# Moving the scaling and transposes of state-space tiles between hops, and dropping one tile of the convolution column, in a hybrid decoder layer

## The chip, the cores and the metric

The kernel runs on one core of one Trainium2 chip. The core has TensorE (PE in the profile, with its weight loads as PEld), VectorE (DVE), ScalarE (ACT), GpSimd (POOL) and SyncE (SP), which issues nearly all transfers. The metric is the device time in microseconds of one execution. A profiled execution is a separate one and has a time of its own.

## The reference

One layer with `S = 2048` tokens and a model width of 1024, in float32. The input is normalized and modulated, projected in one matrix, and split into two groups of heads: attention in a sliding window, and a Mamba-2 state-space group (SSD). The outputs of both are concatenated and projected back; then follows a SwiGLU network. The part that the change touches is the second group:

```python
xbc = silu(causal_depthwise_conv(xbc, conv_w, conv_b))      # four taps along the tokens
xs, Bm, Cm = split(xbc, ...)
...                                                          # chunks of 128 tokens
cb = einsum('bclgn,bcsgn->bclsg', Cc, Bc)
y_diag = einsum('bclsg,bclsgj,bcsgjp->bclgjp', cb, decay, xdt)
states = einsum('bclgn,bclgj,bclgjp->bcgjpn', Bc, decay_to_end, xdt)
...                                                          # prev: the state carried from chunk to chunk
y_off = einsum('bclgn,bcgjpn,bclgj->bclgjp', Cc, prev, exp(a_cs))
y = (y_diag + y_off).reshape(b, s, SSM_HEADS, SSM_HEAD_DIM)
y = y + xf * d_skip[:, None]
y = y * silu(z)
yg = y.reshape(b, s, SSM_GROUPS, 256)
y = yg * rsqrt(mean(yg * yg, axis=-1) + EPS) * ssm_norm_w
out = concatenate([attn, y]) @ w_out
```

## The kernel before, in words

The tokens are worked in four blocks of 512, each of four tiles of 128. A block goes through the projections for query, key, value, convolution (`convolved`) and gate (`gated`), then through attention and the state space, then through the output projection (`out_proj`). The SwiGLU part fills the rest of the span, from about 700 us on, and the mixing of the last two blocks runs beside its beginning.

**Dense work and sides.** The projections are the dense work. A product in float32 is made of three matmuls of split operands (L286 to L288); a column of the convolution takes 24 matmuls, in two pieces of 12 with a `yield` behind each. They write into four PSUM banks named `d`. Attention (`attentions`) and the state space (`ssds`) are sides: Python generators whose `yield`s cut them into hops. After each piece of dense work `tick(ratio)` adds a ratio to a counter, `due`, and issues one hop for each whole unit in it. The ratios are MIX, MIX2 and MIX1. `both` alternates the hops of attention and of the state space. So the program's text, by the order of pieces and hops, sets the order of the instructions of PE, which is kept as written. On the other engines a scheduler orders the instructions with list priorities; hops are issued at high priority (`urgent`), and `behind(engine)` puts an instruction after the last one of an engine issued so far. In the trace an engine's instructions run in that order, so one that waits holds up those behind it.

**The banks of the sides.** The sides have one PSUM bank each for the names `am`, `at`, `sm` and `st`. A state-space tile of 128 tokens uses `st` for its input transposes (L764), for the transposes of B (L778), for the product with the carried state, `yo` (L797), for the new state (L806), and for the transposes of the finished tile (L751 in `turned`). It uses `sm` for the C times B products (L771), for the decays (L735 and L736, with the exponent L738 on ACT and the product L740 on DVE), and for the diagonal part, `yd` (L818). So a matmul into `st` waits until the last reader of the bank before it is done: for L751 this reader is ACT's L754.

**A tile's end.** After L818 DVE adds and gates (L820, L821), ACT squares (L825), and a reciprocal root is found in steps, on POOL for three tiles of a block and on DVE for the last (L249 to L266). Its result scales the tile (`normed`, L746 on ACT), PE transposes the scaled tile (`turned`, L751), ACT evicts it (L754), and SP stores it to `mix`. The finished tile of one step is scaled and turned during the hops of the next step; the last of a block at the block's end.

**The convolution column.** `convolved` computes 8 columns of 128 channels. For each, ACT copies the bank (L507), ACT makes the first tap (L510), DVE adds the fourth from the bank and so frees it (L511), ACT and DVE make the two other taps (L512, L513), POOL adds both (L514). Half a column later `end` takes the tanh on ACT (L499), combines it on DVE (L501) and stores the column (L502 on SP). The tiles come from rings, whose oldest tile is reused when its last reader is done: `s` of three tiles (two per column before), shared with `gated`, and `sx` of two. At L278 ACT rounds weights, at L368 it squares the input of a later block's norm.

**The end of block 1.** The mixing of block 1 (`mix1`) runs beside dense work of blocks 2 and 3 with ratio MIX1. `finish(mix1)` issues all hops that are left, one behind the other, without dense work between. `mixed` loads the mixed tiles back for the output projection and splits them (L848 on ACT, L849 on DVE).

Of the kernel before, what the change touches and what calls it, by code (L numbers as in the profile page):

```python
# [22 lines left out]
T = 512  # L23
# [7 lines left out]
NEG = -1e30  # L31
RAW, SPLIT = 5, 6
TMP, M1, M2, M4 = 8, 3, 8, 4
MIX, MIX2, MIX1, RATIO_UP = 0.78, 1.1, 1.25, 0.75
URGENT = 1000
HALF = 32
ROPE_THETA = 10000.0
# [8 lines left out]
def hymba_layer(ctx, tc, xT, xtok, pos, wada, wadk, vecs, rows, wq, wkv, wz, wx, wo, wgu, wd, outT):  # L46
# [11 lines left out]
    def big(tag, bufs, dt=F32, pool=sb):  # L58
        return pool.tile([P, T], dt, name=tag, tag=tag, bufs=bufs)
# [434 lines left out]
    def convolved(b, h):  # L494
        ending = []

        def end(c, cv, th, o):
            with behind(mybir.EngineType.Activation):
                nc.scalar.activation(th, cv, AF.Tanh)  # L499
            with behind(mybir.EngineType.DVE):  # L500
                nc.vector.scalar_tensor_tensor(o, th, 1.0, cv, ALU.add, ALU.mult)  # L501
            nc.sync.dma_start(xs_d[b][c], o)  # L502

        def evicted(c, ps):
            cin = small([P, T + 3], "cin", 2, pool=ip)
            nc.gpsimd.tensor_copy(cin[:, 0:3], halo[:, c, :])
            nc.scalar.copy(cin[:, 3:T + 3], ps)  # L507
            nc.gpsimd.tensor_copy(halo[:, c, :], cin[:, T:T + 3])
            cv, th, o = big("s", 3, pool=fw), big("s", 3, pool=fw), big("sx", 2, pool=ip)
            nc.scalar.activation(cv, cin[:, 0:T], AF.Identity, scale=conv_w[:, c, 0:1], bias=conv_b[:, c:c + 1])  # L510
            nc.vector.scalar_tensor_tensor(cv, ps, conv_w[:, c, 3:4], cv, ALU.mult, ALU.add)  # L511
            nc.scalar.activation(th, cin[:, 1:1 + T], AF.Copy, scale=conv_w[:, c, 1:2])  # L512
            nc.vector.scalar_tensor_tensor(th, cin[:, 2:2 + T], conv_w[:, c, 2:3], th, ALU.mult, ALU.add)  # L513
            nc.gpsimd.tensor_tensor(cv, cv, th, ALU.add)  # L514
            return c, cv, th, o

        for c in range(8):
            ps = dense()
            for half in range(2):
                if half:  # L520
                    if ending:
                        end(*ending.pop())
                    yield
                whi, wlo = weight(wx[c, half], T, ("x", c, half), b == 1)
                for i in range(4):
                    k = 4 * half + i
                    ws = slice(i * P, (i + 1) * P)
                    mm3(ps, whi[:, ws], wlo[:, ws], h[k][0], h[k][1], k == 0, k == KT - 1)
            with urgent():
                ending.append(evicted(c, ps))  # L530
            if c == 7:
                end(*ending.pop())
            yield
# [176 lines left out]
    def ssds(b, stepping, m):  # L710
        def load(t):
            xl = m.m4().bitcast(F32).rearrange("p h t -> p (h t)").rearrange("p (c t) -> p c t", c=8)
            z, ts = m.m2(), slice(t * P, (t + 1) * P)
            nc.sync.dma_start(xl, xs_d[b][:, :, ts].rearrange("c p t -> p c t"))
            nc.sync.dma_start(z, z_d[b * NT + t])
            return [xl[:, c, :] for c in range(8)], z
# [7 lines left out]
        def factors(t, g):  # L724
            hs, u = slice(4 * g, 4 * g + 4), m.m4()
            uhi, ulo = u[:, 0, :], u[:, 1, :]
            nc.vector.tensor_tensor(uhi.rearrange("p (h l) -> p h l", h=4), ub,
                                    ahi[:, t, hs].bitcast(F32).unsqueeze(2).broadcast_to([P, 4, P]), ALU.mult)
            nc.gpsimd.tensor_tensor(ulo.rearrange("p (h l) -> p h l", h=4), ub,
                                    alo[:, t, hs].unsqueeze(2).broadcast_to([P, 4, P]), ALU.mult)  # L730
            return uhi, ulo

        def decays(u, cbt):
            sg = bank("sm", 1)
            nc.tensor.matmul(sg, later_r, u[0], start=True, stop=False)  # L735
            nc.tensor.matmul(sg, later_r, u[1], start=False, stop=True)  # L736
            dm = m.m2()
            nc.scalar.activation(dm, sg, AF.Exp)  # L738
            d3 = dm.rearrange("p (h l) -> p h l", h=4)
            nc.vector.tensor_tensor(d3, d3, cbt.unsqueeze(1).broadcast_to([P, 4, P]), ALU.mult)  # L740
            return dm
# [6 lines left out]
        def turned(y, o, ts):  # L748
            ps = bank("st", 1)
            for c in range(4):  # L750
                nc.tensor.transpose(ps[:, c * P:(c + 1) * P], y[:, c * P:(c + 1) * P], ident)  # L751
            o3 = o.rearrange("p (c t) -> p c t", c=4)
            for c in range(4):
                nc.scalar.activation(o3[:, c, :], ps[:, c * P:(c + 1) * P], AF.Copy, scale=snw[:, c:c + 1])  # L754
            nc.sync.dma_start(dst[4:8, :, ts].rearrange("c p t -> p c t"), o3)

        for t in range(NT):
# [22 lines left out]
            nc.scalar.copy(btok, ps[:, 0:2 * P])  # L780
            ms = [decays(u, cbt[:, 0, :])]
            u = factors(t, 1)
            if out:
                normed(out[0], out[3])
            yield
            if out:
                turned(*out[:3])
                yield
            ms.append(decays(u, cbt[:, 1, :]))
            if t + 1 < NT:  # L790
                nxt = load(t + 1)
            old = carry["state"]
            if old is not None:
                y = m.m2()
                yo = bank("st", 1)
                for g in range(2):
                    nc.tensor.matmul(yo[:, g * 256:(g + 1) * 256], x[6 + g], old[:, g * 256:(g + 1) * 256],  # L797
                                     start=True, stop=True)
                nc.vector.tensor_tensor(by_head(y), by_head(yo), bc64(ecs), ALU.mult)
                nc.gpsimd.tensor_tensor(y, y, xsd, ALU.add)  # L800
            else:
                y = xsd
            yield
            st = bank("st", 1)
            for g in range(2):
# [23 lines left out]
            rsqrt(rs, ss, 2, nc.vector if t == NT - 1 else nc.gpsimd, "rss", sb)  # L829
            out = (y, o, ts, rs)  # L830
            yield
        yield
        normed(out[0], out[3])
        yield
        turned(*out[:3])
        yield

# [671 lines left out]
    def finish(last):  # L1509
        while last in sides:  # L1510
            if next(sides[0], sides) is sides:
                sides.pop(0)
# [25 lines left out]
    def take(g, n):  # L1538
        for _ in range(n):
            next(g)  # L1540

    with tc.manual_schedule(engines={mybir.EngineType.PE}):
# [42 lines left out]
        h = nxt  # L1585
        run(queries(3, h), MIX1)
        run(keys_values(3, h), MIX1)
        mix = []
        finish(mix1)
        sides.append(attentions(2, common))  # L1590
        conv = convolved(3, h)
        widening.close()
        early = ctx.enter_context(ExitStack())
        bp = early.enter_context(tc.tile_pool(name="b0", bufs=1, reuse_waits="tile"))
# [1 line left out]
        ops = {}  # L1596
        operand_tiles(ops, bp, ("b11",), 12)
        for i in range(6):
            take(conv, 1)
            tick(0.5)  # L1600
            if i > 1:
                next(split, None)
            if i == 1:
                dg = diagonal(y_of[0])
            if i == 3:
                bcs = [spread(y_of[0], bc=side_bank(2), dg=dg)]
# [205 lines left out]
```

## Time and profile before

| what | value |
|---|---|
| time, median of 3 runs | 2202.72 us (2201.24 to 2203.47) |
| profiled execution, its own time | 2204.92 us |
| its span, first to last instruction | 2203.2 us |
| mean granted clock of TensorE | 0.987 |
| ACT busy | 1014.0 us (46%) |
| POOL busy | 550.6 us (25%) |
| share of PE in the chain that ended last | 84% |

The profile gives the busy time of each engine, a line of slices of the span, the chain of work that ended last, and groups of instructions with what ended the idle time before them. A row of the timeline gives the start, the duration, the engine, the line of the kernel and the tiles written and read; in brackets stand the idle time of the engine ahead of it and the instruction that released it. "PE d L286 <- DVE s L511" reads: PE's matmul of line 286, into a bank of `d`, waited for DVE's instruction of line 511, which writes a tile of the ring `s`. The granted clock is the share of TensorE's full speed that it was allowed.

### The profile page before, as it was taken

Reading aid. Unit: us, or ns where it says so; the run is one execution under the profiler, and the core shown is the slowest. Engines: PE = TensorE matmul, PEld = TensorE weight load, DVE = VectorE, ACT = ScalarE, POOL = GpSimd, SP = SyncE. Lnnn points to the kernel's source line nnn. Section 1 sums busy time; section 2 is a strip of 40 time slices with the busy share of each in tenths; the row PEclk is TensorE's granted clock in tenths of the full one; section 3 lists DMA queues with packets and bytes.
Section 4 is the critical chain, followed back from the end, with each engine's and each line's share of the span. In section 5 each row is a group of like instructions: output and inputs, shape, how many; then the busy total and the mean of one; then the engine's idle time right before and its main releaser. Section 6 shows DMA issues by size and latency. Waiting matters only on the chain.

```text
span 2203.2 us, 33249 instructions
## 1 busy us (share of the span) xinstructions
PE 2149.3 (98%) x10984; PEld 1771.8 (80%) x10984; DVE 1661.3 (75%) x3195; ACT 1014.0 (46%) x2135; POOL 550.6 (25%) x658
## 2 busy tenths in 40 slices
PE   8989998999999999999999999999999999999998
PEld 6878896878778677788888788788888888788887
DVE  7978856786668877688888668878888775786575
ACT  3675734653545654443334445533333334554441
POOL 0214432322102211153341221323332321210011
PEclk8999999999999999999999999999999999999999
DMA  7788987796998522333334577735555436678553
GB/s 284 245 298 308 360 260 260 248 360 205 344 345 297 167 90 87 125 106 117 117 116 164 196 264 268 271 127 189 173 165 191 158 120 224 233 264 278 182 163 103
DMA packets 287708, 466.76 MB, mean 212 GB/s; under 512 B 27440, under 2 KB 97072, under 8 KB 287536
## 3 DMA queue, kind: packets, MB, share of 16 engines
q1 hardware_dynamic: 286960, 464.13, 62.7%
q8 instruction: 86, 1.41, 0.3%
q14 instruction: 86, 0.70, 0.1%
q10 hardware_dynamic: 576, 0.52, 0.1%
HBM read 329.73 MB, written 134.81 MB: 211 GB/s over the span
## 4 chain that ended last, share of the span: by engine, by line
PE 84%; DVE 7%; DMA 5%; issue 2%; ACT 2%; POOL 1%; SPq 0%; DVEq 0%; ACTq 0%; POOLq 0%
PE d L1179 18%; PE d L1049 9%; PE d L1048 9%; PE d L1047 9%; PE d L286 6%; PE d L288 6%; PE d L287 6%; PE d L1320 1%; PE am L1049 1%; PE am L1047 1%; PE am L1048 1%; PE am L706 1%; PE sm L1049 1%; PE sm L1047 1%; PE sm L1048 1%
## 5 line engine op out<-in xcount | busy, mean ns | idle before, releaser
L1179 PE MATMUL d<-a,w 128*128 128x512 f32 x1716 | 403.7, 396 | 3.0 <-DVE w L1175 2.1
L1179 PEld LDWEIGHTS d<-a,w 128*128 128x128 f32 x1716 | 321.9, 188 | 81.9 <-DVE w L1175 2.9
L1049 PE MATMUL d<-b,w 128*128 128x512 f32 x924 | 368.1, 399 | 1.4 <-DVE w L896 1.4
L1048 PE MATMUL d<-b,w 128*128 128x512 f32 x924 | 368.5, 399 | 0.2 <-DVE b L930 0.2
L1047 PE MATMUL d<-b,w 128*128 128x512 f32 x924 | 366.5, 400 | 1.7 <-ACT w L895 0.9
L1047 PEld LDWEIGHTS d<-b,w 128*128 128x128 f32 x924 | 175.1, 189 | 41.9 <-ACT b L929 1.6
L1049 PEld LDWEIGHTS d<-b,w 128*128 128x128 f32 x924 | 174.7, 189 | 42.2 <-DVE w L896 2.1
L1048 PEld LDWEIGHTS d<-b,w 128*128 128x128 f32 x924 | 175.3, 190 | 41.3 <-DVE b L930 0.9
L895 ACT ACTIVATE w<-s 128x512 fp32r<-128x512 f32 x176 | 111.0, 631 | 206.1 <-PE d L1049 152.7
L286 PE MATMUL d<-w,hl 128*128 128x256 f32 (+1 forms) x592 | 173.7, 293 | 6.9 <-DVE s L511 6.5
L287 PE MATMUL d<-w,hl 128*128 128x256 f32 (+1 forms) x592 | 168.3, 284 | 0.0
L288 PE MATMUL d<-w,hl 128*128 128x256 f32 (+1 forms) x592 | 168.2, 284 | 0.0
L896 DVE TENSOR_TENSOR w<-s,w 128x512 fp32r<-128x512 f32 x176 | 156.7, 891 | 10.1 <-ACT w L895 9.4
L895 ACT ACTIVATE w<-raw 128x512 fp32r<-128x512 f32 x132 | 83.4, 632 | 151.7 <-PE d L1049 62.1
L1161 DVE TENSOR_TENSOR a<-a 128x512 fp32r<-128x512 f32 x154 | 108.0, 714 | 51.6 <-ACT a L1160 51.2
L1175 DVE TENSOR_TENSOR w<-raw,w 128x512 fp32r<-128x512 f32 x156 | 115.4, 749 | 41.0 <-ACT w L1174 40.8
L296 POOL TENSOR_TENSOR acc<-acc,t 128x512 f32<-128x512 f32 x35 | 53.3, 1523 | 355.8 <-ACT t L295 346.0
L1160 ACT ACTIVATE a<-a 128x512 fp32r<-128x512 f32 x154 | 95.4, 628 | 86.2 <-DMA a<-act_t 48.5
L286 PE MATMUL d<-hl,w 128*128 128x512 f32 x320 | 133.2, 416 | 0.0
L288 PE MATMUL d<-hl,w 128*128 128x512 f32 x320 | 127.0, 397 | 0.3 <-DVE w L279 0.3
L287 PE MATMUL d<-hl,w 128*128 128x512 f32 x320 | 126.7, 396 | 0.0
L1174 ACT ACTIVATE w<-raw 128x512 fp32r<-128x512 f32 x156 | 90.2, 587 | 78.7 <-PE d L1179 53.0
(421 smaller groups left out, 4778.2 us busy)
## 6 DMA issues: line engine op xcount, KB each, us to landing
raw<-in_wgu_dram SPq DMA_DIRECT2D x176, 256.0 KB, 2.9
act_t<-t SPq DMA_DIRECT2D x88, 256.0 KB, 3.1
a<-act_t SPq DMA_DIRECT2D x88, 256.0 KB, 4.4
act_b<-t SPq DMA_DIRECT2D x66, 256.0 KB, 2.0
a<-act_b SPq DMA_DIRECT2D x66, 256.0 KB, 4.5
aw<-in_wada_dram SPq DMA_DIRECT2D x64, 256.0 KB, 4.9
w<-w_x SPq DMA_DIRECT2D x32, 512.0 KB, 6.0
raw<-wd_s SPq DMA_DIRECT2D x64, 256.0 KB, 3.1
```

Source lines behind the costliest of these rows:

```text
L286: nc.tensor.matmul(out, ahi, bhi, start=first, stop=False)
L287: nc.tensor.matmul(out, ahi, blo, start=False, stop=False)
L288: mm3.last = nc.tensor.matmul(out, alo, bhi, start=False, stop=last)
L895: nc.scalar.activation(hi, x, AF.Copy)
L896: eng.tensor_tensor(lo, x, hi.bitcast(F32), ALU.subtract)
L1047: nc.tensor.matmul(out, ahi, bhi, start=first and k == 0, stop=False, skip_group_check=True)
L1048: nc.tensor.matmul(out, ahi, blo, start=False, stop=False, skip_group_check=True)
L1049: mm3.last = nc.tensor.matmul(out, alo, bhi, start=False, stop=k == 3, skip_group_check=True)
L1160: nc.scalar.activation(hi, raw, AF.Copy)
L1161: nc.vector.tensor_tensor(lo, raw, hi.bitcast(F32), ALU.subtract)
L1175: nc.vector.tensor_tensor(w[1], raw, w[0].bitcast(F32), ALU.subtract)
L1179: mm3.last = nc.tensor.matmul(ps, w[x][:, ws], act[k][y], start=new and k == 0 and x + y == 0, stop=k == KP - 1 and x == 1, skip_group_che ...
```

## The change

The diff makes four edits.

1. In `ssds` the scaling of the tile before (`normed`) moves a hop later, to stand with the product with the carried state (`yo`), and `turned` a hop later again, to stand with the second decay and the load of the next tile. A tile's hops were: input; B, first decay and `normed`; `turned`; second decay, load and `yo`; new state; diagonal part. They are: input; B and first decay; `normed` and `yo`; `turned`, second decay and load; new state; diagonal part. The first tile of a block, which has no tile before it, has one hop more. At a block's end two hops pass before `normed` and two before `turned`, where one did.
2. In `convolved` the tile `th` is gone. The taps two and three and the tanh are computed in place in `o`, which comes from the ring `sx` of two. The ring `s` of three holds one tile per column in place of two.
3. MIX1 goes from 1.25 to 1.5.
4. In place of `finish(mix1)` stands a loop that takes pieces of the fourth block's convolution, with a tick after each, as long as `mix1` has hops; pieces taken there are left out of the six that follow.

```diff
-MIX, MIX2, MIX1, RATIO_UP = 0.78, 1.1, 1.25, 0.75
+MIX, MIX2, MIX1, RATIO_UP = 0.78, 1.1, 1.5, 0.75
...
-        def end(c, cv, th, o):
+        def end(c, cv, o):
             with behind(mybir.EngineType.Activation):
-                nc.scalar.activation(th, cv, AF.Tanh)
+                nc.scalar.activation(o, cv, AF.Tanh)
             with behind(mybir.EngineType.DVE):
-                nc.vector.scalar_tensor_tensor(o, th, 1.0, cv, ALU.add, ALU.mult)
+                nc.vector.scalar_tensor_tensor(o, o, 1.0, cv, ALU.add, ALU.mult)
...
-            cv, th, o = big("s", 3, pool=fw), big("s", 3, pool=fw), big("sx", 2, pool=ip)
+            cv, o = big("s", 3, pool=fw), big("sx", 2, pool=ip)
...
-            nc.scalar.activation(th, cin[:, 1:1 + T], AF.Copy, scale=conv_w[:, c, 1:2])
-            nc.vector.scalar_tensor_tensor(th, cin[:, 2:2 + T], conv_w[:, c, 2:3], th, ALU.mult, ALU.add)
-            nc.gpsimd.tensor_tensor(cv, cv, th, ALU.add)
-            return c, cv, th, o
+            nc.scalar.activation(o, cin[:, 1:1 + T], AF.Copy, scale=conv_w[:, c, 1:2])
+            nc.vector.scalar_tensor_tensor(o, cin[:, 2:2 + T], conv_w[:, c, 2:3], o, ALU.mult, ALU.add)
+            nc.gpsimd.tensor_tensor(cv, cv, o, ALU.add)
+            return c, cv, o
...
             u = factors(t, 1)
+            yield
             if out:
                 normed(out[0], out[3])
-            yield
-            if out:
-                turned(*out[:3])
-                yield
-            ms.append(decays(u, cbt[:, 1, :]))
-            if t + 1 < NT:
-                nxt = load(t + 1)
             old = carry["state"]
             if old is not None:
                 y = m.m2()
...
             else:
                 y = xsd
+            yield
+            if out:
+                turned(*out[:3])
+            ms.append(decays(u, cbt[:, 1, :]))
+            if t + 1 < NT:
+                nxt = load(t + 1)
             yield
             st = bank("st", 1)
...
-        yield
+        for _ in range(2):
+            yield
         normed(out[0], out[3])
-        yield
+        for _ in range(2):
+            yield
         turned(*out[:3])
...
-        mix = []
-        finish(mix1)
+        mix, conv, begun = [], convolved(3, h), 0
+        while mix1 in sides:
+            take(conv, 1)
+            tick(1.0)
+            begun += 1
         sides.append(attentions(2, common))
-        conv = convolved(3, h)
...
         for i in range(6):
-            take(conv, 1)
+            if i >= begun - 2:
+                take(conv, 1)
             tick(0.5)
```

Three places show how the instructions move. The numbers in the names tell tiles apart; "..." stands for dense matmuls left out, and a line of the changed kernel is about two higher than the same line before, from L845 on, or six lower for `yo` (L791 for L797).

The first is the end of the first block's convolution on ACT: the copy L507, the taps L510 and L512, with the weights' rounding L278, the norm's squares L368 and, of the attention, L624 and L631. Before:

```order
L278 ACTIVATE w<-raw 128x512
L368 ACTIVATE t,ssq<-t 128x512
L507 COPY cin<-d 128x512
L278 ACTIVATE w<-raw 128x512
L624 CAST k_ring<-am 128x128
L368 ACTIVATE t,ssq<-t 128x512
L631 ACTIVATE m_1569<-at 128x512
L368 ACTIVATE t,ssq<-t 128x512
L499 ACTIVATE s<-s 128x512
L368 ACTIVATE t,ssq<-t 128x512 x2
L512 ACTIVATE s<-cin,vec 128x512
L510 ACTIVATE s<-cin,vec 128x512
```

And with the change:

```order
L512 ACTIVATE sx<-cin,vec 128x512
L507 COPY cin<-d 128x512
L278 ACTIVATE w<-raw 128x512
L510 ACTIVATE s<-cin,vec 128x512
L278 ACTIVATE w<-raw 128x512
L512 ACTIVATE sx<-cin,vec 128x512
L368 ACTIVATE t,ssq<-t 128x512
L278 ACTIVATE w<-raw 128x512
L368 ACTIVATE t,ssq<-t 128x512
L624 CAST k_ring<-am 128x128
```

The last column's copy and taps now stand ahead of the squares and of the attention's copies, and the tap L510 ahead of L512.

The second is the last tile of block 0. On PE, before, the transposes of the tile before it (`m_3919`) and of the tile itself (`m_4545`):

```order
L751 MATMUL st<-ident,m_3919 128x128 x4
...
L735 MATMUL sm<-m_4336,later_r 128x512
L736 MATMUL sm<-m_4336,later_r 128x512
L797 MATMUL st<-state,m_3915 128x256 x2
...
L806 MATMUL st<-m_4225,m_4328 128x256 x2
...
L818 MATMUL sm<-m_4223,m_4333 128x64 x4
L818 MATMUL sm<-m_4223,m_4542 128x64 x4
...
L751 MATMUL st<-ident,m_4545 128x128 x4
```

With the change the same tiles are `m_3883` and `m_4512`:

```order
L791 MATMUL st<-state,m_4009 128x256 x2
...
L751 MATMUL st<-ident,m_3883 128x128 x4
L735 MATMUL sm<-m_4454,later_r 128x512
L736 MATMUL sm<-m_4454,later_r 128x512
...
L806 MATMUL st<-m_4300,m_4446 128x256 x2
L818 MATMUL sm<-m_4298,m_4451 128x64 x4
L818 MATMUL sm<-m_4298,m_4560 128x64 x4
...
L751 MATMUL st<-ident,m_4512 128x128 x4
```

Between the last L818 and the last L751 stood 24 dense matmuls and now stand 60. The transposes of the tile before moved the other way, to 12 dense matmuls ahead of L806, and L806 and L818 have none between them. The same place on ACT, with the change (`m_4178` is the tile that L751 of `m_3883` transposes into, `m_4560` the decay that the second L818 reads):

```order
L499 ACTIVATE sx<-s 128x512
L850 ACTIVATE hl_5240<-hl_5240 128x512
L507 COPY cin<-d 128x512
L754 ACTIVATE m_4178<-st,vec 128x128 x4
L850 ACTIVATE hl_5242<-hl_5242 128x512
L738 ACTIVATE m_4560<-sm 128x512
L510 ACTIVATE s<-cin,vec 128x512
```

Before, both L754 of that tile and the exponent L738 stood ahead of the first split (L848, now L850); now they stand behind the first and the second.

The third is a tile of block 1 that has one before it, on PE. Before, from the diagonal part of a tile to its transposes (`m_6105`), the attention's hops (L623, L628, L663, L697) left out where they only repeat:

```order
L818 MATMUL sm<-m_5890,m_6098 128x64 x4
...
L764 MATMUL st<-ident,m_6101 128x128 x4
L771 MATMUL sm<-m_6101 128x128 x2
...
L778 MATMUL st<-ident,m_6101 128x128 x2
L735 MATMUL sm<-m_6323,later_r 128x512
L736 MATMUL sm<-m_6323,later_r 128x512
...
L697 MATMUL at<-ident,m_5839 128x128 x4
L751 MATMUL st<-ident,m_6105 128x128 x4
```

With the change (`m_6061`):

```order
L818 MATMUL sm<-m_5905,m_6115 128x64 x4
...
L764 MATMUL st<-ident,m_6118 128x128 x4
L771 MATMUL sm<-m_6118 128x128 x2
...
L778 MATMUL st<-ident,m_6118 128x128 x2
...
L706 MATMUL am<-m_6379,v_ring 64x256 x4
...
L791 MATMUL st<-state,m_6118 128x256 x2
...
L751 MATMUL st<-ident,m_6061 128x128 x4
L735 MATMUL sm<-m_6403,later_r 128x512
```

The product with the carried state and the second decay changed places around L751, and 72 dense matmuls stand between L818 and L751 where 48 stood.

## The prediction

> **What bounds the kernel now.** I read the page's busy times and its clock line first, then the waits of PE, then windows, then the timeline at the longest waits.
>
> ```profile
> PE 2149.3 (98%) x10984; PEld 1771.8 (80%) x10984; DVE 1661.3 (75%) x3195; ACT 1014.0 (46%) x2135; POOL 550.6 (25%) x658
> PEclk8999999999999999999999999999999999999999
> ```
>
> TensorE is busy for 98% of the span, and the change adds and removes no matmul. So the time can only move by TensorE's waits and by what the clock does around them. Busy time includes matmuls at half clock, which is why 98% hides some of the loss. In the waits the columns are total, count and longest.
>
> ```profile
> PE st L751 <- ACT m L746: 11.8, 2, 7.5
> PE d L286 <- DVE s L511: 6.5, 1, 6.5
> ...
> PE d L287 <- DVE b L849: 1.6, 2, 1.3
> ```
>
> The two longest lines stand where the change edits: the transposes of a finished SSD tile (L751) wait for its scaling (L746), and a projection (L286) waits for a conv column's eviction (L511). The windows show the price (columns: width; PE, PEld, DVE, ACT, POOL busy; granted clock; DMA share; GB/s).
>
> ```profile
> 100.00:150.00 50.00, 42.13 (x276) 37.68 (x276) 42.06 (x106) 37.64 (x90) 11.82 (x17) 0.93 0.80 279
> 350.00:400.00 50.00, 42.48 (x203) 33.90 (x203) 35.12 (x80) 24.77 (x59) 16.05 (x20) 0.90 0.67 222
> 450.00:500.00 50.00, 50.00 (x284) 40.10 (x284) 40.10 (x90) 26.30 (x68) 11.24 (x21) 1.00 0.98 346
> 500.00:550.00 50.00, 45.49 (x356) 42.18 (x355) 28.95 (x122) 18.15 (x53) 14.39 (x34) 0.97 0.64 207
> 700.00:750.00 50.00, 45.28 (x199) 33.79 (x199) 39.13 (x74) 29.42 (x68) 12.43 (x9) 0.86 0.60 201
> ```
>
> TensorE idles 7.9, 7.5, 4.5 and 4.7 us in four of these windows, and in the same four the clock is below 1. Only the first three lie at what is edited.
>
> **Change part by part.** It moves hops; the instructions of a tile stay the same. The tanh tile of the conv is gone as a name, not as work.
>
> *(a) The last tile of block 0.* The rows are of PE, ACT and DVE.
>
> ```profile
> 348.52 1.89 PE L818 MATMUL sm<-m,m 128*128 128x64 f32 x16
> 363.52 1.11 PE L751 MATMUL st<-ident,m 128*128 128x128 f32 x4 [7.53 <-ACT m L746]
> 369.46 0.39 PE L286 MATMUL d<-hl,w 128*128 128x512 f32 x1
> 369.69 0.40 PE L287 MATMUL d<-hl,w 128*128 128x512 f32 x1
> ...
> 348.12 0.63 ACT L848 ACTIVATE hl<-hl 128x512 fp32r<-128x512 f32 x1 [5.57 <-DMA hl<-mix]
> 362.96 0.91 ACT L746 ACTIVATE m<-m,rs 128x256 f32<-128x256 f32 x2 [3.87 <-DVE rs L266]
> 364.67 1.15 ACT L754 ACTIVATE m<-st,vec 128x128 f32<-128x128 f32 x4 [0.28 <-PE st L751]
> 342.06 1.51 DVE L740 TENSOR_TENSOR m<-m,m 128x512 f32<-128x512 f32 x1
> ```
>
> L751 was due at 363.52 − 7.53 = 355.99. Behind the wait the clock is half until about 369.3 (the 0.90 of the window; from 369.46 on matmuls start 0.23 us apart again): of the 5.8 us from 363.52 to there half is lost, 2.9. Together 10.4 us. Now 60 dense matmuls stand between L818 and L751 where 24 stood: 36 × 0.23 = 8.3 us more, against 7.53 needed. This wait goes, with 0.8 us to spare.
>
> But something is late next. L751 of the tile before now stands 12 dense matmuls ahead of L806, which takes the same single bank (st) and so waits until ACT's L754 has emptied it. On ACT that L754 stands behind L850 (L848 of before), which the 348.12 row shows waiting 5.57 us for a transfer. If this lands as before: 348.12 + 0.63 (L850) + 0.57 (the conv copy) + 1.15 (L754), less overlap, gives about 350.3, while L806 is due about 1 us ahead of 348.52. That is a wait of 2.8. Then L818 needs DVE's L740, whose exponent (L738) stands on ACT behind a second L850: 350.3 + 0.6 + 0.6 + 1.5 = 353.0, while L818's second half is due near 352.3 or before: 0.7 to 2.7, taken as 1.8. New stall 4.6; at half clock behind it for 3.4 us another 1.7. Queued behind both is all of TensorE. Term (a): −7.5 − 2.9 + 4.6 + 1.7 = **−4.1** (from −10.4 if the transfer lands 5 us sooner, to 0 if it lands 4 us later).
>
> *(b) A tile of block 1.*
>
> ```profile
> 489.94 1.89 PE L818 MATMUL sm<-m,m 128*128 128x64 f32 x16
> 508.63 0.90 PE L751 MATMUL st<-ident,m 128*128 128x128 f32 x4 [4.26 <-ACT m L746]
> ...
> 508.07 0.91 ACT L746 ACTIVATE m<-m,rs 128x256 f32<-128x256 f32 x2 [0.97 <-POOL rs L261]
> ```
>
> L751 was due at 504.4. From the end of L818 (491.8) to that of L746 (509.0) the chain over POOL's root takes 17.1 us. Now 72 dense matmuls instead of 48 lie between L818 and L751, 24 × 0.23 = 5.5 us more, over 4.26: the wait goes, with the clock's part (0.03 of 50 us, 1.5, or 3.4 us at half, 1.7). I leave 0.5 for the closer rows around it. Term (b): **−5.5** (−6.0 to −4).
>
> *(c) The conv column at 122.*
>
> ```profile
> 115.75 0.28 PE L286 MATMUL d<-w,hl 128*128 128x256 f32 x1
> 129.11 0.58 PE L286 MATMUL d<-w,hl 128*128 128x256 f32 x1 [6.47 <-DVE s L511]
> ...
> 120.44 0.63 ACT L368 ACTIVATE t<-t 128x512 f32<-128x512 f32 x1 [1.31 <-DMA t<-in_xtok_dram]
> 121.55 0.63 ACT L278 ACTIVATE w<-raw 128x512 fp32r<-128x512 f32 x1
> 127.47 0.80 ACT L510 ACTIVATE s<-cin,vec 128x512 f32<-128x512 f32 x1
> 128.31 0.75 DVE L511 SCALAR_TENSOR_TENSOR s<-d,vec,s 128x512 f32<-128x512 f32 x1
> ```
>
> The column's matmuls are done near 116, yet L510 runs at 127.47: ahead of it on ACT stand L368, which waits for a transfer, and L512, which waits for a tile of the three-tile ring. L286 was due at 122.64. In the new order L507 comes ahead of L368, and between it and L510 stands one L278. At worst that runs where it does now: 121.55 + 0.63 + 0.80 + 0.75 = 123.7, a stall of 1.1; with the hand-overs 1.5, and 0.8 for a short half clock. Of 6.47 + 2.35 (4.7 us at half, from 129.1 to 133.8, in which the 0.93 of the window lies) = 8.8 remain 2.3. Term (c): **−6.5** (−8.8 to −3).
>
> *(d), (e) The last hops of block 2's projections and the denser ticks.* With MIX1 at 1.5 every second tick issues two hops beside `gated(2)`, `out_proj(0)`, `queries(3)` and `keys_values(3)`, so that block 1's mixing is used up before `finish(mix1)` stood. The loop in its place therefore runs no conv piece (`mix1` has left `sides`), and `begun` stays 0: the edit along conv pieces costs and brings nothing by itself. What `finish` packed together waited, and the loads behind it too:
>
> ```profile
> 556.61 1.08 PE L706 MATMUL am<-m,v_ring 128*64 128x256 f32 x8 [0.88 <-ACT m L699]
> ```
>
> With part of the 1.6 us of L849 above, −1.9. Against it stand two hops at one tick (L706 waiting for L699 as here: two or three times 0.9) and ACT queued behind an L512 that now waits for a store; I take **+2.0**, from 0 to +8. The region from 741 us on keeps its order nearly to the row; the idle of 700 to 750 I leave unchanged, ±4.
>
> *The ring of two.* The column's third tap and tanh now live in `o`, so L512 of a column waits until the store of the column two before has landed, instead of DVE's L511 and L501 of columns before.
>
> ```profile
> 201.82 0.59 ACT L507 COPY cin<-d 128x512 f32<-128x512 f32 x1 [4.46 <-PE d L288]
> 217.27 0.59 ACT L507 COPY cin<-d 128x512 f32<-128x512 f32 x1
> 219.21 0.71 ACT L512 ACTIVATE s<-cin,vec 128x512 f32<-128x512 f32 x1
> ...
> 231.49 1.02 SPq L502 DMA_DIRECT2D xs<-sx  x1
> ...
> DMA to landing us min/median/max: 2.0/5.2/8.3
> ```
>
> Two columns take 217.27 − 201.82 = 15.45 us; a tile of `o` would be held from 219.21 until 231.49 + 5.2 = 236.69, 17.5 us. But the half column's delay of tanh is in it, TensorE has four banks ahead, and L510 and L511, which free the bank, now need only the other ring. I cost it within (e), and its failure as a rival.
>
> Sum: −4.1 − 5.5 − 6.5 − 1.9 + 2.0 = −16.0. The profiled execution took 2204.9, the span's 2203.2 and 1.7 outside it, 2.2 above the median of the runs; so 2188.9 as a profile and **2187** as a median.
>
> On the clock a rule speaks. These rows stand ahead of half clock in the 700 window:
>
> ```profile
> 699.13 0.50 PE L1047 MATMUL d<-b,w 128*128 128x512 f32 x1 [0.92 <-ACT w L895]
> 701.33 0.79 PE L1049 MATMUL d<-b,w 128*128 128x512 f32 x1 [0.38 <-DVE w L896]
> 702.35 0.63 PE L1048 MATMUL d<-b,w 128*128 128x512 f32 x1
> 702.78 0.63 PE L1049 MATMUL d<-b,w 128*128 128x512 f32 x1
> ```
>
> Matmuls start 0.43 us apart after waits of 0.92 and 0.38, so short waits in a row of small matmuls can halve the clock too; that is why I charge 1.7 behind the split stall of (a). The Trainium skill, page "TensorE: Matmul & The Clock Gate", section "Why this matters for your kernels", warns of idle gaps over about 3 us alone. By that rule the stall of (a), split into 2.8 and 1.8, would keep the clock and the time would be 2185; the row disagrees with the rule here.
>
> **The rivals.** *No new waits:* if the transfer ahead of L850 lands sooner and the ticks of two hops find their operands, everything named goes: −10.4 − 6.0 − 8.8 − 2.5 = −27.7, 2175. For it: those transfers are issued by the same hops and the DMA share is 0.67 there. Against: two hops now share a tick at the place of (a).
>
> *Given back to the transfers:* the stages before 650 us move 200 to 350 GB/s, with a DMA share of 0.98 in 450 to 500. Where TensorE gains, weights may come no sooner, and a wait for raw weights takes each gain's place: 2199 to 2203. Against: in that very window TensorE is busy for all 50.00 us.
>
> *The ring of two sets the pace (slower):* 17.5 − 15.45 = 2.0 us per pair of columns, three pairs a block, four blocks: +24; with the −16 and the cover of four banks lost, up to 2211. It decides from the point where a store lands later than 3.2 us after its issue in a column that has no slack; the median is 5.2. It would show as L286 <- L511 in every block. Against: 4.46 us of ACT's idle ahead of L507 in the row above, which is slack the ring may use.
>
> **How the numbers follow.** The likeliest case, with 2181 to 2195 from the bounds of (a), (c) and (e), has 0.62; no new waits 0.14; given back 0.13; the ring 0.11. A measurement of this kernel can tell about 0.2%, 4.4 us, from no change. Faster than that: 0.62 + 0.14 and a little of the third, 0.79; the same 0.12; slower 0.09, since the ring's loss may stay below the gain. The range for eight in ten reaches from the second case to the third: 2175 to 2200.
>
> **What would show it.** Right: no L751 <- L746 over 1 us among the waits of PE, a clock of 0.97 or more in 350 to 400 and 500 to 550, L286 <- L511 at 122 below 2 us, and L806 or L818 with a wait of 2 to 5 us near 347. Wrong: L512 waiting for `sx` over 2 us in most columns with L511 among PE's releasers; a new line of PE for `raw` or `w`; or the last TURN at later than its 60 rows.

## The result

| | before | changed |
|---|---|---|
| median of 6 runs | 2202.51 us (2201.24 to 2203.9) | 2190.07 us (2188.52 to 2192.3) |
| profiled execution, its own time | 2204.92 us | 2188.96 us |
| its span | 2203.2 us | 2186.9 us |

The ratio is 0.9942, with a 95% interval of 0.9932 to 0.9952. The forecast was 2187 us. The medians differ by 12.4 us and the two profiled executions by 16.0, because the profile before was 2.4 us above its median and the one after 1.1 below. The terms of the prediction were worked out from profiles, so they are held against the profiles below; by the medians, some 3.5 us of what those show belong to these two executions and not to the change.

The page after, its busy times and clock:

```profile
PE 2140.5 (98%) x10984; PEld 1763.5 (81%) x10984; DVE 1669.6 (76%) x3195; ACT 1017.8 (47%) x2137; POOL 547.5 (25%) x658
PEclk8999999999999999999999999999999999999999
```

As many matmuls, 8.8 us less of busy time: they ran less at half clock. The waits of PE after (total, count, longest):

```profile
PE am L663 <- DVE k_ring L625: 4.8, 2, 4.7
...
PE d L1049 <- ACT t L1081: 3.0, 1, 3.0
PE d L286 <- DVE s L511: 2.7, 1, 2.7
PE at L628 <- DMA m<-q: 2.4, 2, 2.1
...
PE st L806 <- ACT m L754: 0.4, 1, 0.4
```

L751 for L746, the longest wait of before (11.8 us), is not among them. L511's has fallen from 6.5 to 2.7. New are the scores (L663) waiting for the split of the keys (L625) and, at 711 us, L1049; the wait for a load of queries (L628) has grown from 0.9 to 2.1. The windows after:

```profile
100.00:150.00 50.00, 43.42 (x299) 38.58 (x298) 47.20 (x126) 39.41 (x94) 13.16 (x15) 1.00 0.95 328
350.00:400.00 50.00, 48.22 (x284) 40.70 (x282) 37.85 (x90) 31.71 (x74) 16.93 (x24) 1.00 0.81 272
400.00:450.00 50.00, 45.83 (x295) 38.94 (x295) 40.02 (x99) 29.48 (x78) 12.69 (x21) 0.97 0.80 266
500.00:550.00 50.00, 50.00 (x392) 46.27 (x390) 28.92 (x125) 16.40 (x48) 11.61 (x28) 1.00 0.79 264
700.00:750.00 50.00, 46.82 (x229) 35.52 (x230) 44.70 (x81) 32.05 (x73) 14.74 (x11) 0.97 0.52 169
```

The clock, 0.93, 0.90, 0.97 and 0.86 in four of these windows before, is 1.00 in three and 0.97 in that from 700. What is gained from 350 to 400 and from 500 to 550 is partly lost again in the window from 400 to 450, whose TensorE was busy for 48.2 us at full clock before.

Where the 16.3 us of the span went is seen from the same instruction in both traces (starts in us):

| instruction | before | after | lead so far |
|---|---|---|---|
| first conv copy (L507) of block 0 | 75.8 | 75.9 | -0.1 |
| first conv copy of block 1 | 201.8 | 198.4 | 3.4 |
| first conv copy of block 2 | 337.0 | 333.3 | 3.7 |
| fifth conv copy of block 2 | 375.9 | 361.9 | 14.0 |
| first conv copy of block 3 | 563.5 | 550.4 | 13.1 |
| first matmul of the SwiGLU quads | 693.3 | 680.6 | 12.7 |
| first matmul of the down projection | 1318.8 | 1303.0 | 15.8 |
| end of the span | 2203.2 | 2186.9 | 16.3 |

So 10.3 us came at the end of block 0's mixing, 3.5 about the convolution of block 0, 3.1 in the transition behind 693 us, and nothing between 376 and 563 us, where 4.3 us of wait had gone and 0.9 us of the lead was lost.

### The profile page after: what moved, and what is told of

It reads as the page before. It is cut to its first block, busy times and chain, and to the rows that moved or that the text cites. A ratio compares the mean times of both kernels' runs of the same rounds, so it can differ in the third digit from the quotient of the medians.

```text
span 2186.9 us, 33266 instructions
## 1 busy us (share of the span) xinstructions
PE 2140.5 (98%) x10984; PEld 1763.5 (81%) x10984; DVE 1669.6 (76%) x3195; ACT 1017.8 (47%) x2137; POOL 547.5 (25%) x658
## 4 chain that ended last, share of the span: by engine, by line
PE 79%; DVE 9%; DMA 6%; ACT 3%; issue 3%; POOL 1%; SPq 0%; DVEq 0%; ACTq 0%; POOLq 0%
PE d L1181 15%; PE d L1049 9%; PE d L1050 9%; PE d L1051 9%; PE d L286 5%; PE d L287 5%; PE d L288 5%; PE d L1322 1%; PE am L1051 1%; PE am L1049 1%; PE am L1050 1%; PE am L706 1%; DMA a<-act_t 1%; PE sm L1051 1%; PE sm L1050 1%
## 5 line engine op out<-in xcount | busy, mean ns | idle before, releaser
L1049 PE MATMUL d<-b,w 128*128 128x512 f32 x924 | 366.1, 399 | 5.0 <-ACT t L1081 3.0
L1049 PEld LDWEIGHTS d<-b,w 128*128 128x128 f32 x924 | 174.1, 188 | 45.2 <-ACT t L1081 3.5
L897 ACT ACTIVATE w<-s 128x512 fp32r<-128x512 f32 x176 | 110.9, 632 | 203.2 <-PE d L1051 146.0
L286 PE MATMUL d<-w,hl 128*128 128x256 f32 (+1 forms) x592 | 172.1, 291 | 2.7 <-DVE s L511 2.7
L1177 DVE TENSOR_TENSOR w<-raw,w 128x512 fp32r<-128x512 f32 x156 | 109.8, 713 | 39.0 <-ACT w L1176 37.0
L286 PE MATMUL d<-hl,w 128*128 128x512 f32 x320 | 131.6, 411 | 0.3 <-DVE stp L565 0.3
```

What stands on the lines that cost most here:

```text
L286: nc.tensor.matmul(out, ahi, bhi, start=first, stop=False)
L897: nc.scalar.activation(hi, x, AF.Copy)
L1049: nc.tensor.matmul(out, ahi, bhi, start=first and k == 0, stop=False, skip_group_check=True)
L1177: nc.vector.tensor_tensor(w[1], raw, w[0].bitcast(F32), ALU.subtract)
```

## The experiments

Each kernel is the kernel before or the changed one with the edit given.

### One edit alone

The first edit of the change alone (the hops in `ssds`):

> The kernel before with the first edit alone (the hops of the state-space tiles). My theory: the two waits of L751 for L746 and the half clock behind them go (10.4 and 6.0 us), the wait of L286 for L511 at 122 us stays (6.5 us and 2.4 of clock), the wait of the attention's scores (L663) for the keys' split (L625) appears where four hops stand without dense work between (4.7 and 1.7 us), and finish(mix1) still packs four hops (about 2 us): in sum 8 us under the kernel before, about 2194.5. Rival, that the gain came from the conv column's ring and the ticks: within 2 us of the kernel before.

Measured: 2190.7 us, ratio 0.9947 (0.9933 to 0.9961). That is the changed kernel's time within the intervals. L751's wait for L746 is gone, L511's is there, and the scores wait:

```profile
PE d L286 <- DVE s L511: 6.6, 1, 6.6
PE am L663 <- DVE k_ring L625: 4.6, 1, 4.6
```

The first edit carries the whole gain. I had expected 4 us less of it.

The conv column alone:

```diff
...
-            cv, th, o = big("s", 3, pool=fw), big("s", 3, pool=fw), big("sx", 2, pool=ip)
+            cv, o = big("s", 3, pool=fw), big("sx", 2, pool=ip)
...
```

> The kernel before with the second edit alone (no tile for the tanh). The order on PE is that of before. My theory: the wait of L286 for L511 at 122 us falls from 6.5 to about 2.7 us and loses its half clock, the waits of L751 stay at 7.5 and 4.3: 3 to 5 us under the kernel before, about 2198.5. Rival, that the ring of two sets the convolution's pace: L512 waits for the store of sx in most columns, and the time is not under that of before.

Measured: 2204.68 us, ratio 1.0007 (0.9998 to 1.0016), no difference. My theory fell on the time, though its wait at L286 came out as expected. PE's waits in the stage, and SP's issue of the load of queries, in this run:

```profile
127.54 0.39 PE L286 MATMUL d<-w,hl 128*128 128x256 f32 x1 [2.80 <-DVE s L511]
...
145.67 0.63 PE L628 MATMUL at<-ident,m 128*128 128x128 f32 x4 [2.96 <-DMA m<-q]
...
138.82 0.98 SPq L612 DMA_DIRECT2D m<-q  x1
```

and before:

```profile
146.04 0.63 PE L628 MATMUL at<-ident,m 128*128 128x128 f32 x4 [0.93 <-DMA m<-q]
...
140.76 0.48 SPq L612 DMA_DIRECT2D m<-q  x1
```

The load is issued 1.9 us sooner and lands when it did: it takes 6.7 us, not 5.1 (by the view of DMA issues of that stretch), where the transfers' share from 130 to 140 us is 1.04 and was 0.73. L628 starts at 145.7 against 146.0. This is the rival "given back to the transfers", in one stage: of what TensorE won at L286, 2.0 us go into the longer wait at L628, and the clock falls behind it (0.85 from 140 to 150 us, 1.00 before). It doesn't account for all of it: this profile reached L286 2.1 us later than that of before (due at 124.7 against 122.6), by a later start that the last section comes to. Measured from its own first conv copy, it is still 1.6 us ahead at the first of block 1, and no longer ahead at the first of block 3.

The ratio alone:

> The kernel before with the third edit alone (MIX1 of 1.5). My theory: L751's and L511's waits stay, what finish packed at 556 us (0.9) goes, four hops in a row still cost about 2 us, and the half clock from 700 to 711 us may go with the other place of attentions(2): 0 to 5 us under the kernel before, about 2200. Rival, that the denser ticks brought the most of the gain: 8 us or more under it.

Measured: 2202.01 us, ratio 0.9995 (0.9986 to 1.0005), no difference that can be told, within what was expected. But the waits are other ones than I named: 3.5 us of L286 at 563 us, at the convolution of block 3, and two of 1.2 and 1.3 us ahead of it, from 554 to 557 us; against them, L751's later wait, which I had left standing, fell from 4.3 to 1.4 us. This place comes back below.

### The parts of the first edit

> The kernel before with the shift of the hops within a tile alone; at a block's end one hop before normed and one before turned, as before. 36 dense matmuls lie between L818 and the last L751 of block 0, not 60. My theory: 24 fewer at 0.23 us take away the 1.7 us to spare and leave a wait of L751 for L746 near 3.8 us at 360 us, with some half clock behind it; the wait at 508 us is gone. The four hops in a row now are the second decay, the scores, the new state and the probabilities' transposes, which wait for the softmax, 3 to 5 us. In sum 2 to 6 us under the kernel before, about 2199. Rival, that the shift within the tile carries the gain of both waits: 10 us or more under it.

Measured: 2187.68 us, ratio 0.9935 (0.992 to 0.995). The wait is as worked out:

```profile
362.40 1.11 PE L751 MATMUL st<-ident,m 128*128 128x128 f32 x4 [3.28 <-ACT m L746]
```

But the four hops in a row cost only 1.4 us (L697), not 3 to 5, and the rival's time came out. The shift within the tile without the block's two extra hops is as fast as the whole edit or faster.

> The kernel before with the block's end alone (two hops before normed, two before turned). 48 dense matmuls between L818 and the last L751 of block 0. My theory: 24 more at 0.23 us leave 7.5 - 5.5 = 2.0 us of the wait at 360 us and no half clock; the later wait of a tile in block 1 (4.3 us) stays, unless its place moves; the four hops in a row are the keys' transposes, the new state, the scores and the diagonal part, so the wait of L663 for L625 appears (3 to 5 us). In sum 2 to 6 us under the kernel before, about 2198. Rival, that the block's end carries the whole gain: 10 us or more under it.

Measured: 2194.22 us, ratio 0.9959 (0.9945 to 0.9974), between the time of the theory and that of the rival. L751's wait in block 0 is 0.99 us where 2.0 was worked out, and at the four hops in a row L663 waits twice, 2.7 and 0.8 us, with half clock behind it. The later wait of L751, which was to stay, is not there; one of 1.6 us stands elsewhere. So each part alone takes more than half of block 0's wait and leaves 3.28 or 0.99 of 7.53 us; which hops fall together later differs between them, and the times with it.

### The four ticks in a row

The new wait of the changed kernel at 403 us, on PE, ACT and DVE:

```profile
397.15 0.27 PE L623 MATMUL am<-ident,m 128*128 128x128 f32 x1
...
402.99 0.35 PE L663 MATMUL am<-k_ring,m 64*128 64x256 f32 x1 [4.66 <-DVE k_ring L625]
...
397.85 0.24 ACT L624 CAST k_ring<-am 128x128 fp32r<-128x128 f32 x1
...
397.03 2.13 DVE L851 TENSOR_TENSOR hl<-hl 128x512 fp32r<-128x512 f32 x2
...
400.88 1.75 DVE L208 CUSTOM_DVE_ANT_0 aw<-aw,csil,vec 128x512 f32<-128x512 f32 x1
...
402.56 0.28 DVE L625 TENSOR_TENSOR k_ring<-am,k_ring 128x128 fp32r<-128x128 f32 x1
```

The keys' transposes (L623) and the scores that need them (L663) are two of four hops issued in a row behind four pieces of `gated(2)`. Between them lies no dense work, and L625 stands on DVE behind splits, roundings and two products. Before, the hops that fell there were scores, diagonal part, transposes of probabilities and the next tile's input, and the place cost 1.8 us. The experiment puts one tick behind each piece:

```diff
-        take(g, 4)
         for _ in range(4):
+            take(g, 1)
             tick(MIX2)
```

> The changed kernel, and the four pieces of gated(2) that are taken in a row ahead of four ticks now have one tick behind each. My theory: the wait of L663 for L625 at 403 us (4.66 us, and 1.7 of half clock behind it) was the keys' transposes and the scores issued without dense work between; it goes, and the time is 6 us under the changed kernel, about 2184. Rival: DVE is late there by the splits of the mixed tiles (L851) and the rounding of weights, whichever hop waits, so the wait moves to another hop and the time stays within 2 us of the changed kernel.

Measured: 2184.03 us, ratio 0.9907 (0.9894 to 0.9921): 6.0 us under the changed kernel, as expected. The windows of that kernel:

```profile
350.00:400.00 50.00, 49.67 (x291) 42.21 (x290) 39.76 (x92) 29.97 (x72) 19.30 (x25) 1.00 0.78 262
400.00:450.00 50.00, 47.53 (x315) 40.00 (x314) 41.71 (x104) 32.48 (x89) 12.37 (x20) 1.00 0.88 300
```

It is faster than both kernels. The same with the first edit alone:

> The kernel before with the first edit and the four ticks put between the four pieces of gated(2); the conv column's tile, MIX1 and finish as before. My theory: the first edit carries the gain, the others bring nothing: 6.4 us under the run with the first edit alone, 2184 to 2185, as the changed kernel with the ticks between. Rival, that ring, ratio or loop bring something once the wait at 403 us is gone: 3 us or more over that kernel's 2184.0.

Measured: 2192.05 us, ratio 0.995 (0.9935 to 0.9965); the rival came out, 8 us over. L663's wait is gone here too, but three others stand in its place: L806 1.8 us at 349 us, L706 2.0 at 417 and L697 3.2 at 435, the last two with half clock behind them:

```profile
PE am L706 <- ACT m L699: 4.7, 4, 2.0
...
PE am L697 <- DVE ast L672: 3.2, 1, 3.2
```

The ring is not what makes the difference: a kernel below with the first edit, the ratio and these ticks, but without the ring, takes 2183.15 us, and the loop runs empty there. So it is the ratio, which brings nothing alone, that decides here into which places the same hops fall.

### Without the ring, without the ratio

> The changed kernel with the conv column as before (its own tile for the tanh). My theory: the wait of L286 for L511 at 122 us is back at 6.5 us with its half clock, and the wait for the query's load (L628) behind it shrinks from 2.1 to about 1 us, since the load lands at the same time either way: 0 to 4 us over the changed kernel, 2190 to 2194. Rival, that the ring costs elsewhere what it saves there: at or under the changed kernel's 2190.1.

Measured: 2192.25 us, ratio 0.9947 (0.9933 to 0.9962). L286 waits 5.9 us again, L628 1.1; the time is 2.2 us over the changed kernel, within the intervals.

> The changed kernel with the ticks between the pieces of gated(2), and the conv column as before. My theory: 0 to 4 us over the kernel with the ticks between (2184.0), by the wait at 122 us alone. Rival: no difference, the transfers behind it take the gain back.

Measured: 2183.15 us, ratio 0.9908 (0.9892 to 0.9924), no difference to the kernel with the ticks between. In three comparisons the ring's tile makes no difference that can be told in the time. In the traces it does shorten its own stage: from the first conv copy of block 0 to that of block 1 it takes 122.0 to 124.4 us in the five runs with the edited column, and 124.9 to 126.7 in the eight without (the run with one tile, below, left out).

> The changed kernel with MIX1 at 1.25 as before, so that block 1's mixing still has hops where the loop stands, and the loop takes conv pieces along with them. My theory: the loop does no more than finish did with its waits (0.9 us at 556 us): within 3 us of the changed kernel, about 2190. Rival, that the ratio of 1.5 carries part of the gain: 4 us or more over the changed kernel.

Measured: 2201.33 us, ratio 0.9993 (0.9983 to 1.0003). My theory fell: 11 us over the changed kernel. PE at the first matmul of `out_proj(1)`:

```profile
578.48 0.79 PE L286 MATMUL d<-b,w 128*128 128x512 f32 x1 [5.80 <-ACT b L850]
```

The window around it in this run, and behind it the same window of the changed kernel:

```profile
550.00:600.00 50.00, 42.95 (x202) 32.12 (x201) 31.17 (x81) 27.33 (x63) 7.52 (x13) 0.90 0.82 278
```

```profile
550.00:600.00 50.00, 48.12 (x236) 36.44 (x235) 35.89 (x96) 29.44 (x72) 5.72 (x9) 1.00 1.00 354
```

Here the loop of the fourth edit runs. It uses up conv pieces, and these are then missing between the end of block 1's mixing and `out_proj(1)`, which needs its tiles loaded and split: 12 dense matmuls stand there, where the kernel before has 72. The loads are issued at 572.0 us, L850 gets the first at 577.8, and TensorE waits; with the half clock behind it the lead over the kernel before falls from 13.4 us at block 3's first conv copy to 3.9 at its fifth. A ratio of 1.5 keeps the loop from running at all: block 1's mixing ends at 541 us there, ahead of the last of `keys_values(3)`.

The run of the first edit alone has the ratio of 1.25 too, with `finish` where this one has the loop, and takes 2190.7 us. There the mixing ends at 550.0 us, here at 565.9. Besides the loop the two differ by the ring, which made no difference elsewhere. So the 11 us come with the loop, not with the lower ratio as such.

> The changed kernel with the ticks between the pieces, and at a block's end one hop before normed and one before turned as before. My theory: the wait of L751 for L746 at 360 us is back with 3.3 us, as in the run with the shift alone, and nothing else of size: 2 to 5 us over the kernel with the ticks between, 2186 to 2189. Rival, that the block's end only moves phases: no difference, or under 2184.

Measured: 2198.38 us, ratio 0.9972 (0.9962 to 0.9982), 14 us over the kernel with the ticks between; my theory fell here too. L751's wait is only 1.1 us, but two other stalls stand in the trace. At the end of block 0 L806 waits, and the clock is half for 6.8 us behind it:

```profile
348.27 0.63 ACT L848 ACTIVATE hl<-hl 128x512 fp32r<-128x512 f32 x1 [6.09 <-DMA hl<-mix]
...
349.27 1.15 ACT L754 ACTIVATE m<-st,vec 128x128 f32<-128x128 f32 x4
350.56 1.49 PE L806 MATMUL st<-m,m 128*128 128x256 f32 x4 [2.10 <-ACT m L754]
```

This kernel is 1.4 us behind that with the ticks between at block 2's first conv copy and 8.8 at the fifth. By block 3's first it is 19.5 behind, mostly by this:

```profile
558.99 0.76 PE L286 MATMUL d<-hl,w 128*128 128x512 f32 x1 [7.01 <-DVE stp L559]
...
544.44 3.22 SPq L843 DMA_DIRECT2D b<-mix  x5
...
553.66 3.15 SPq L274 DMA_DIRECT2D w<-w_x  x5
```

L286 here is the first matmul of block 3's convolution. Its weights (`w_x`, L274) were issued on SP behind the loads of block 1's mixed tiles (L843) and landed at 558.9 us by the trace; the releaser named, on DVE, is not the cause. In the changed kernel SP issues the first `w_x` at 536 us and these loads at 553.9. Without the two extra hops, and with the ratio of 1.5, block 1's mixing ends 144 dense matmuls ahead of the next hops of the sides, and its loads go ahead of the weights; in the changed kernel it ends 72 ahead of them. In the run of the ratio alone, where L286 waits 3.5 us at this place, SP's order is the same: the mixed tiles from 544.3 us on, the first `w_x` at 557.4. So the ratio and the block's extra hops pull the end of this mixing in opposite directions, and the changed kernel's pair of them misses both stalls: that of an end so early that the loads go ahead of the weights, and that of an end so late that the loop runs.

### The ring as a bound

```diff
-            cv, o = big("s", 3, pool=fw), big("sx", 2, pool=ip)
+            cv, o = big("s", 3, pool=fw), big("sx", 1, pool=ip)
```

> The changed kernel with one tile in the ring sx, not two. A column's tile is then held from L512 over half a column (3.9 us), the tanh and the product (some 2 us) to the landing of its store (4.5 us), about 10.5 us, against 7.7 us that a column takes. My theory, that two tiles are enough and one is not: L512 waits for the store in most columns, TensorE waits for L511, 2.8 us a column, 50 to 90 us over the changed kernel. Rival, that L512's wait is hidden by the four banks even so: within 10 us of the changed kernel.

Measured: 2246.34 us in one run, 56 us over the changed kernel. PE's waits, then those of ACT:

```profile
PE d L286 <- DVE s L511: 36.6, 7, 8.5
...
ACT sx L512 <- DMA xs<-sx: 37.3, 14, 4.2
```

and ACT's in the changed kernel, with two tiles:

```profile
ACT sx L512 <- DMA xs<-sx: 5.0, 3, 3.1
```

L512 waits for the store in 14 of 32 columns, not in most. The time is within what my theory gave, in a single run. The mechanism of the third rival is real, but with two tiles it is small: three waits on ACT, none of which shows as a difference in the time.

## Why the prediction was right, and where only the sum was

The time lay within the range and near the forecast, and the two waits of L751 went for the reason given. But the terms did not come out as they were set: (a) gave 6 us more than its figure, (b) and (c) gave less, and the errors cancelled. That the sum of 16.0 us is also what the two profiles differ by is luck. Of the four signs named for being right two came out (no wait of L751 for L746, a clock of 1.00 in both windows); L286 waits 2.7 us and not under 2, and L806 0.4 us and not 2 to 5.

**(a), set at -4.1, was -10.3.** The wait and its half clock went, as worked out from 36 more matmuls; L751 starts without a wait. The step that failed is the new stall: 4.6 us and 1.7 of clock were set for L806 and L818, and it is 0.43:

```profile
342.72 0.63 ACT L850 ACTIVATE hl<-hl 128x512 fp32r<-128x512 f32 x1 [4.41 <-DMA hl<-mix]
...
343.73 1.15 ACT L754 ACTIVATE m<-st,vec 128x128 f32<-128x128 f32 x4
...
345.02 1.10 PE L806 MATMUL st<-m,m 128*128 128x256 f32 x4 [0.43 <-ACT m L754]
345.96 1.98 PE L818 MATMUL sm<-m,m 128*128 128x64 f32 x16
...
361.66 0.60 PE L751 MATMUL st<-ident,m 128*128 128x128 f32 x4
```

The chain is the one that was described: the split waits for the transfer, L754 stands behind it, and L806 behind L754. Its size was off first of all by the landing. In the run of the first edit alone, where TensorE reaches this stage 0.3 us behind the kernel before, the load is issued at 343.2 us against 342.9 and lands at 346.5 against 348.1: 3.3 us on the way, not 5.2. L806 was also due 0.7 us later than I had it. The other runs bear this out. In the changed kernel and six others with the new order of hops within a tile, the first of these loads is 3.3 to 3.9 us on the way, and L806 waits 0.7 us at most. In three it is 5.1 to 5.6 us on the way (the first edit with the ticks between, the run without the block's extra hops, and that with one tile of `sx`), and L806 waits 1.8 to 2.1 us. L818's part of the stall, set at 1.8, came in none of them. I had taken one landing time of before as given, though the range of the term (transfer 5 us sooner or 4 later) said what it hung on. The run of the shift alone confirms the other half of the term: 24 matmuls fewer than in the changed kernel leave 3.28 us of wait, worked out 3.8.

**(b), set at -5.5, went, and was given back elsewhere.** From 500 to 550 us TensorE is busy for 50.00 us at full clock. But the same edit moved the keys' transposes next to their scores in the four ticks in a row, 4.66 us and some 1.7 of half clock. The prediction has no term for that place: which hops were to fall there, and the chain between them, was not worked out. The run with the ticks between shows the price of that place in the changed kernel, 6.0 us.

**(c), set at -6.5, was -3.5 at most and nothing that can be told as a time.** The wait of L286 fell to 2.75 us, set 1.5, and its half clock went. What is left of it does not stand where the term had it, on ACT:

```profile
118.66 0.80 ACT L510 ACTIVATE s<-cin,vec 128x512 f32<-128x512 f32 x1
...
120.60 2.06 DVE L344 SCALAR_TENSOR_TENSOR hl<-t,mod,hl 128x512 fp32r<-128x512 f32 x3
122.58 0.68 DVE L279 TENSOR_TENSOR w<-raw,w 128x512 fp32r<-128x512 f32 x1
...
124.55 0.74 DVE L511 SCALAR_TENSOR_TENSOR s<-d,vec,s 128x512 f32<-128x512 f32 x1
```

L510 is done at 119.5 us, where the term had it at worst at 123.0; from there DVE works without a pause on splits and products that stand ahead of L511. The other step that failed is that nothing lay behind the wait: the load of queries does not come sooner, and L628 waits 2.1 us for it where it was 0.9. Where the ring is edited alone, put back, or put back beside the other ticks, the times agree within their intervals.

**(d) and (e), set at +0.1 together, were +0.4** from block 3's first copy to the quads. That stretch holds only their end: the denser ticks begin with `gated(2)`, and what they cost before block 3 is mixed with (b) in the 0.9 us lost there. That the loop runs empty was right, and that it "costs and brings nothing by itself" was right only because the ratio keeps it empty: where it runs the time is 11 us longer.

**The transition, left unchanged with ±4, gained 3.1.** TensorE is busy for 46.8 of 50 us from 700 to 750 as against 45.3, at a clock of 0.97 as against 0.86. It comes out otherwise in nearly every run (its clock is 1.00, 0.90, 1.00 and 0.97 in the runs of hops, ring, ratio and ticks between), and no run here tells which edit moved it.

Of the rivals, the one without new waits holds for (a) alone, the transfers took back a part of (c), and the ring of two did not set the pace.

## What to carry to other kernels

When a wait goes because work is moved, look next at the chain between the instructions that now stand together, and at the queue of transfers ahead of them: here both gave back, within 50 us, a part of what an edit had won. An edit that changes nothing alone can still decide where the others' work falls, so an edit is judged with and without the rest, and that holds for a repair too: spreading out the hops issued in a row brought 6 us beside the ratio of 1.5, and nothing beside the first edit alone.

## What the runs showed of the hardware

The clock fell where I had not expected it, and behind waits that were short. In the kernel with the ticks between:

```profile
681.16 1.08 PE L706 MATMUL am<-m,v_ring 128*64 128x256 f32 x8 [0.30 <-ACT m L699]
682.17 0.97 PE L663 MATMUL at<-k_ring,m 64*128 64x256 f32 x6
683.46 0.50 PE L1049 MATMUL d<-b,w 128*128 128x512 f32 x1 [0.31 <-ACT w L897]
...
685.35 0.51 PE L1051 MATMUL d<-b,w 128*128 128x512 f32 x1 [0.25 <-DVE w L898]
...
687.36 0.63 PE L1050 MATMUL d<-b,w 128*128 128x512 f32 x1
687.79 0.63 PE L1051 MATMUL d<-b,w 128*128 128x512 f32 x1
```

Matmuls start 0.43 us apart behind waits of 0.30, 0.31 and 0.25 us in a stretch with narrow matmuls. In the changed kernel the clock halves behind waits of 4.66 and 3.05 us and stays full behind 2.75; in the run without the block's extra hops it halves behind 2.10, above. The Trainium skill, page "TensorE: Matmul & The Clock Gate", section "Why this matters for your kernels", names idle gaps over about 3 us; the long waits here agree with it, the 2.10 us and the stretch at 685 us lie outside it. What decides there, no run here separates.

Single profiles also differ before the first convolution: the first conv copy starts between 75.5 and 78.2 us in the traces of the changed kernel, the kernel before and the other runs with two tiles of `sx`. The copy comes by 75.9 us in six of them, the changed kernel and the kernel before among these, and not before 77.3 in the seven others. From 7 to 12 us TensorE runs 22 to 26 matmuls in the six and 14 to 16 in the seven. In the six the granted clock reads full for 3.4 us in that stretch and then half until about 28 us; 3.4 us at full clock in place of half are worth 1.7. The seven have no record of the clock ahead of 30 us. Some 2 us of the difference between two profiles can be this alone, which is why the medians carry the verdicts.
